# One decoder layer in float32 on one core: x's first blocks on ACT's queue, the last sums later, the stores in another order

## The chip, the cores and the metric

The kernel runs on 1 of the 8 cores of a Trainium2 chip. The metric is the device time of one execution in microseconds, the median of some runs. A core has five engines with a queue of instructions each: PE (matrix products), DVE and ACT (elementwise work), POOL and SP. Loads and stores are DMAs; SP and ACT issue them on hardware queues of their own (here called SP's and ACT's queue), POOL on a software queue. A DMA instruction stands in its engine's instruction stream like any other. SP does nothing but issue DMAs; ACT also computes.

## What is computed

One step of a hybrid decoder layer for 320 tokens: 256 of a prompt (two row tiles of 128) and 64 of a sample (8 sequences of 8), with D = 2048 columns, all in float32.

```python
def decoder_layer(x, conv_prev, k_win, v_win, rel_bias, w_in, w_conv, w_conv_out, sinks,
                  w_attn_out, w_o, g_mix, g_ffn, w_gate, w_up, w_down):
    xn = rms_norm(x, g_mix)
    z = xn @ w_in                       # B, C, h, q, k, v, gate_conv, gate_attn
    u = c_gate * h_conv
    y_conv = (b_gate * short_conv(u)) @ w_conv_out
    y_attn = window_attention(q, k, v, rel_bias, sinks) @ w_attn_out
    merged = jax.nn.sigmoid(gate_c) * y_conv + jax.nn.sigmoid(gate_a) * y_attn
    h = x + merged @ w_o
    hn = rms_norm(h, g_ffn)
    return h + (jax.nn.silu(hn @ w_gate) * (hn @ w_up)) @ w_down

y = rms_norm(h, g_final)                # and the new k, v and conv states
```

## The kernel before, in words

**Products.** Every product has the tokens as the moving side: a matmul takes a 128x128 block of weights and 128x320 of x, transposed so that the columns of x lie on partitions. To keep float32's precision, both sides are split in two parts of a shorter format: a weight tile `raw` becomes `hi` (a copy on ACT, L93) and `lo` (the rest, a subtraction on DVE, L94), x becomes `xh` and `xl` in the same way, and each product is three matmuls: hi by xh, hi by xl, lo by xh. `product` (L116) does that for all products but the first, with weight tiles that SP loads (`load_cols`, L96). Weights pass once: the kernel streams some 250 MB through four buffers of raw tiles and three each of `hi` and `lo`.

**The first product** is the one for k and v (`kv_product`, L267). It has four accumulators (c = 0 to 3) and sixteen steps kc, one for each 128 columns of x, with 12 matmuls a step. Its weight tiles are loaded by `load_kv` (L256) on SP: one step each for the first two (256 KB), then two steps each (512 KB).

**x.** The three row tiles `xs[t]` (two of the prompt, one of the sample) are loaded in five blocks of columns, `XB = [2, 2, 4, 4, 4]` times 128 columns, by `x_load(i)` (L223): three DMAs a block. In the following the load of block i and row tile t is x[i,t]; blocks 0 and 1 have 128 KB for a row tile of the prompt and 64 KB for the sample's, the others twice that. Block 0 is loaded ahead of all, x[0,1] on ACT's queue and the others on SP's; `g_mix`, as `vrow`, follows on ACT's. Blocks 1 to 4 are issued by `kv_product` on SP behind the weight tiles that `x_after` names. `x_prep(kc)` (L242) does what a step needs: three transposes on PE into one PSUM tile `pt`, then `xh` on ACT (scaled by `g_mix`), `xl` on DVE, and a plain copy `hT` on DVE for the residual. It is called for steps 0 and 1 at step 0, for 2 and 3 at step 1, then two steps ahead. Nine matmuls on constants (L235) keep PE busy before x is there.

**The order of the work.** The kernel is written with a layer that sets all semaphores and puts the instructions of each engine in order: of what is ready by its own reckoning, the earliest written goes first. `after(marks)` (L71) pins what is written under it behind a marked instruction of the same engine, in issue order only. Loads on the two hardware queues share eight completion semaphores, which are handed out in turn.

```python
with after(*((vecs_in,) if k0 == 0 else mark[k0])):
    split_to(hi[:, :n, :], lo[:, :n, :], raw[:, :n, :])
```

These two lines of `load_kv` (L263) pin the split of the first weight tile behind the copy of `g_mix`, and of every other behind the `xh` and `xl` of its first step. Side work (small loads on POOL, squares of x on ACT, the root of the mean square) is put between the tiles of the first product by `tick` (L111).

**The end.** The down product (w_down, `dn`) runs in two halves of its inner dimension. In the second half, each pair of column blocks is added to the residual `hT`, transposed back to rows (`fa`), squared with a row sum on ACT (`row_squares`, L908) into `ssf`, and scaled by `g_final` (`y_part`). The last pair differs. `next_last` (L923) treats column block 14 while PE still works on block 15, and sums the 15 row sums so far into `s15` (L932, L933). After the last matmul, block 15 is added in three parts (L966) and transposed (L967), row tile 0 is squared, and its inverse root `r0` is made (`row_mean`, `inv_root`: one root on ACT, a reciprocal and three small steps on DVE, the last three a Newton step). Row tiles 1 and 2 get theirs together (`r12`). Then all rows are scaled, in parts, by ACT and DVE (`scale`, L979; `scale_last`, L985, for the last two column blocks), and stored (`send`, L993): row tiles 0 and 1 from SP, the sample's 64 rows from ACT, last.

## Time and profile before

| | us |
|---|---|
| runs | 1701.84, 1702.18, 1702.85; median 1702.18 |
| the profiled execution | 1702.27 |
| its span, first to last instruction | 1700.5 |
| PE busy | 1682.2 (99%) |
| DVE, ACT, POOL busy | 863.3 (51%), 643.5 (38%), 81.3 (5%) |
| first matmul of the first product | 8.11 |
| from the last transposes to the end of the span | 13.3 |

A matmul of 128x320 is listed with 0.31 us, but matmuls are pipelined: one starts every 0.147 us while PE is the one that sets the pace (48 take 7.04 us in the chain of work). Idle time of an engine is listed with what ended it. A DMA is listed where it is issued (an engine's name with q), with the time that the issuing took; the time to landing is another view. The profile's clock is that which PE was granted, as a share of full speed. Its DMA numbers are the busy share of the core's 16 DMA engines and the rate in GB/s.

### The profile page before, as it was taken

What the parts mean: (1) busy time and instruction counts of PE and PEld (TensorE: products, weight loads), DVE (VectorE), ACT (ScalarE), POOL (GpSimd) and SP (SyncE); (2) the same over time, 40 slices, a digit from 0 to 9 for tenths busy, and PEclk for the clock granted to TensorE, in tenths of its full rate; (3) what the DMA queues carried; (4) which work ended last, traced back from release to release, by engine and by line L of the source; (5) the groups of instructions that cost most, each with busy time, mean ns of one, the idle gap of its engine ahead of it and who ended that gap; (6) DMA issues with size and microseconds to landing.
All of it is one profiled execution on the core that took longest, in us unless ns stands there. A gap on an engine that the chain in (4) does not pass through costs nothing.

```text
span 1700.5 us, 27713 instructions
## 1 busy us (share of the span) xinstructions
PE 1682.2 (99%) x11600; PEld 1670.9 (98%) x11600; DVE 863.3 (51%) x1231; ACT 643.5 (38%) x945; POOL 81.3 (5%) x127
## 2 busy tenths in 40 slices
PE   8999999999999999999999999999999999999996
PEld 7999999999999999999999999999999999999996
DVE  7667554444444445556454545433345545454443
ACT  6445443333333333334333333322233333333432
POOL 1001221000000001220000000000000000000000
PEclk9999999999999999999999999999999999999998
DMA  7754554555555544444444444444444444445442
GB/s 217 216 153 142 161 151 131 147 150 151 151 152 151 149 149 149 149 149 149 149 149 150 149 150 152 152 152 150 149 150 149 149 149 149 149 151 171 149 140 96
DMA packets 256719, 258.22 MB, mean 152 GB/s; under 512 B 9091, under 2 KB 251615, under 8 KB 256433
## 3 DMA queue, kind: packets, MB, share of 16 engines
q1 hardware_dynamic: 254128, 249.86, 47.8%
q0 software_dynamic: 2128, 5.92, 1.2%
q8 instruction: 91, 1.49, 0.4%
q10 hardware_dynamic: 336, 0.66, 0.2%
q14 instruction: 36, 0.29, 0.1%
HBM read 253.29 MB, written 5.08 MB: 152 GB/s over the span
## 4 chain that ended last, share of the span: by engine, by line
PE 95%; issue 2%; DMA 1%; DVE 1%; SPq 0%; POOL 0%; ACT 0%; DVEq 0%; POOLq 0%; ACTq 0%
PE fg L134 18%; PE fu L134 18%; PE dn L134 18%; PE wo L134 7%; PE ga L134 7%; PE gc L134 7%; PE C L134 3%; PE B L134 3%; PE H L134 3%; PE ya L134 3%; PE yc L134 3%; PE q L134 2%; DMA wraw<-in_w_in_dram 0%; DMA rel<-in_rel_bias_dram 0%; PE po L508 0%
## 5 line engine op out<-in xcount | busy, mean ns | idle before, releaser
L94 DVE TENSOR_TENSOR wlo<-wraw,whi 128x1024 fp32r<-128x1024 f32 (+1 forms) x481 | 573.8, 1195 | 703.9 <-ACT whi L93 701.3
L93 ACT ACTIVATE whi<-wraw 128x1024 fp32r<-128x1024 f32 (+1 forms) x481 | 493.3, 1030 | 852.4 <-PE dn L134 198.2
L134 PE MATMUL dn<-a_h,whi 128*128 128x320 f32 x704 | 218.5, 310 | 0.0
L134 PE MATMUL fu<-hh_t,whi 128*128 128x320 f32 x704 | 217.4, 309 | 0.0
L134 PE MATMUL dn<-a_h,wlo 128*128 128x320 f32 x704 | 217.3, 309 | 0.0
L134 PE MATMUL dn<-a_l,whi 128*128 128x320 f32 x704 | 217.2, 309 | 0.0
L134 PE MATMUL fg<-hh_t,whi 128*128 128x320 f32 x704 | 217.2, 309 | 0.0
L134 PE MATMUL fg<-hl_t,whi 128*128 128x320 f32 x704 | 217.2, 309 | 0.0
L134 PE MATMUL fg<-hh_t,wlo 128*128 128x320 f32 x704 | 217.2, 309 | 0.0
L134 PE MATMUL fu<-hl_t,whi 128*128 128x320 f32 x704 | 217.2, 308 | 0.0
L134 PE MATMUL fu<-hh_t,wlo 128*128 128x320 f32 x704 | 217.2, 308 | 0.0
L134 PEld LDWEIGHTS fu<-hl_t,whi 128*128 128x128 f32 x704 | 132.2, 188 | 0.1
L134 PEld LDWEIGHTS dn<-a_l,whi 128*128 128x128 f32 x704 | 132.2, 188 | 0.0
L134 PEld LDWEIGHTS fu<-hh_t,whi 128*128 128x128 f32 x704 | 132.2, 188 | 0.1
L134 PEld LDWEIGHTS dn<-a_h,whi 128*128 128x128 f32 x704 | 132.2, 188 | 0.0
L134 PEld LDWEIGHTS dn<-a_h,wlo 128*128 128x128 f32 x704 | 132.2, 188 | 0.0
L134 PEld LDWEIGHTS fg<-hh_t,whi 128*128 128x128 f32 x704 | 132.2, 188 | 0.0
L134 PEld LDWEIGHTS fg<-hh_t,wlo 128*128 128x128 f32 x704 | 132.2, 188 | 0.0
L134 PEld LDWEIGHTS fg<-hl_t,whi 128*128 128x128 f32 x704 | 132.2, 188 | 0.0
L134 PEld LDWEIGHTS fu<-hh_t,wlo 128*128 128x128 f32 x704 | 132.2, 188 | 0.0
L134 PE MATMUL gc<-xh_t,whi 128*128 128x320 f32 x256 | 79.6, 311 | 0.0
L134 PE MATMUL ga<-xh_t,wlo 128*128 128x320 f32 x256 | 79.4, 310 | 0.0
(285 smaller groups left out, 2934.7 us busy)
## 6 DMA issues: line engine op xcount, KB each, us to landing
wraw<-in_w_in_dram SPq DMA_DIRECT2D x119, 512.0 KB, 3.6
wraw<-in_w_gate_dram SPq DMA_DIRECT2D x88, 512.0 KB, 3.6
wraw<-in_w_up_dram SPq DMA_DIRECT2D x88, 512.0 KB, 3.6
wraw<-in_w_down_dram SPq DMA_DIRECT2D x88, 512.0 KB, 3.5
wraw<-in_w_o_dram SPq DMA_DIRECT2D x32, 512.0 KB, 3.5
wraw<-in_w_in_dram SPq DMA_DIRECT2D x34, 256.0 KB, 4.4
wraw<-in_w_conv_out_dram SPq DMA_DIRECT2D x16, 512.0 KB, 3.5
wraw<-in_w_attn_out_dram SPq DMA_DIRECT2D x32, 256.0 KB, 4.1
```

The source lines that it names most:

```text
L93: last["hi"] = nc.scalar.activation(hi, src, AF.Copy)
L94: last["lo"] = nc.vector.tensor_sub(lo, src, hi.bitcast(F32))
L134: last["mm"] = nc.tensor.matmul(ps[c][:, :T], w[:, k, c * P:(c + 1) * P], x(kc), start=(kc == 0 and i == 0), stop=(kc == nk - 1 and i == 2),)
```

## The change

It has two parts, one at each end of the kernel.

At the front, blocks 0, 1 and 2 of x are all loaded ahead of the first weight tile in the written order, and on ACT's queue, but for x[0,1], which is on SP's. ACT's queue now has nine loads: x[0,0], `vrow`, x[0,2], then the three of block 1 and of block 2. Blocks 3 and 4 stay on SP. There are seven warm-up matmuls instead of nine. `x_prep(0)` is called ahead of the first product's loop, `x_prep(1)` between the first and second accumulator of step 0, and `x_prep(kc + 2)` ahead of the last accumulator of step kc; the transposes of all but the first are pinned behind the matmul written last. The split of the first weight tile is now pinned behind `xh` and `xl` of step 0, like that of the others.

At the end, `s15` is summed after the three adds of block 15 instead of in `next_last`. The root of row tile 0 is written out, with one of its steps in another form but as many of them. The parts that are scaled and stored change: row tile 0 goes as 512, 512 and 1024 columns instead of 256, 768 and 1024; then the sample's rows, 768 and 1280 columns; then row tile 1, 768 and 1280. All stores are issued by SP.

```diff
--- before.py
+++ after.py
@@ -224,14 +224,17 @@
         cs = slice(sum(XB[:i]) * P, sum(XB[:i + 1]) * P)
         for t, (t0, tn) in enumerate(TOK):
             src = a["x_prompt"][0, t0:t0 + tn, :] if t < 2 else a["x_sample"].flatten_outer_dims()
-            eng = nc.scalar if i == 0 and t == 1 else nc.sync
+            eng = nc.sync if i > 2 or (i, t) == (0, 1) else nc.scalar
             eng.dma_start(xs[t][:tn, cs], src[:, cs])
-
-    x_load(0)
-    nc.scalar.dma_start(vrow[0:16, :], a["g_mix"][0].rearrange("(k p) -> k p", p=P))
+            if (i, t) == (0, 0):
+                nc.scalar.dma_start(vrow[0:16, :], a["g_mix"][0].rearrange("(k p) -> k p", p=P))
+
+
+    for i in range(3):
+        x_load(i)
 
     wm = ps_aux("wm")
-    for _ in range(9):
+    for _ in range(7):
         nc.tensor.matmul(wm, busy[:, :P], busy, start=True, stop=True)
     pv = ps_aux("pv")
     nc.tensor.transpose(pv[:, 0:16], vrow[0:16, :], ident[:16, :16])
@@ -241,8 +244,9 @@
 
     def x_prep(kc):
         pt = ps_aux(u("pt"))
-        for t in range(3):
-            nc.tensor.transpose(pt[:, t * P:(t + 1) * P], xs[t][:, kc * P:(kc + 1) * P], ident)
+        with after(*((last["mm"],) if kc else ())):
+            for t in range(3):
+                nc.tensor.transpose(pt[:, t * P:(t + 1) * P], xs[t][:, kc * P:(kc + 1) * P], ident)
         m1 = nc.scalar.activation(xh_t[:, kc, :], pt[:, :T], AF.Copy, scale=g_mix[:, kc:kc + 1])
         m2 = nc.vector.scalar_tensor_tensor(
             xl_t[:, kc, :], pt[:, :T], g_mix[:, kc:kc + 1], xh_t[:, kc, :].bitcast(F32),
@@ -260,13 +264,14 @@
         )
         hi = wp.tile([P, KT // 2, CK], F32R, tag="whi", name=u("whi"), bufs=3)
         lo = wp.tile([P, KT // 2, CK], F32R, tag="wlo", name=u("wlo"), bufs=3)
-        with after(*((vecs_in,) if k0 == 0 else mark[k0])):
+        with after(*mark[k0]):
             split_to(hi[:, :n, :], lo[:, :n, :], raw[:, :n, :])
         return hi, lo
 
     def kv_product(tiles, x_after):
 
         ps = [ps_acc(u("kv")) for _ in range(4)]
+        x_prep(0)
         k0 = 0
         for i, n in enumerate(tiles):
             hi, lo = load_kv(k0, n)
@@ -277,9 +282,8 @@
                 order.sort(key=lambda kc: kc[1])
             for k, c in order:
                 kc = k0 + k
-                if c == 0:
-                    for j in range(2 * kc, 2 * kc + 2) if kc < 2 else range(kc + 2, min(kc + 3, KC)):
-                        x_prep(j)
+                if (kc, c) == (0, 1) or c == 3 and kc + 2 < KC:
+                    x_prep(1 if c == 1 else kc + 2)
                 for m, (w, x) in enumerate(((hi, xh), (hi, xl), (lo, xh))):
                     last["mm"] = nc.tensor.matmul(
                         ps[c][:, :T], w[:, k, c * P:(c + 1) * P], x(kc),
@@ -363,7 +367,7 @@
         nc.vector.tensor_mul(rbsq, rb, rb)
 
     side_work[0] = start_rest()
-    ps_kv = kv_product([1, 1] + [2] * 7, {0: (1,), 1: (2,), 3: (3,), 4: (4,)})
+    ps_kv = kv_product([1, 1] + [2] * 7, {3: (3,), 4: (4,)})
     for _ in side_work[0]:
         pass
     for c in range(2):
@@ -929,8 +933,6 @@
                 nc.tensor.transpose(pc[0][:tn, t * P:(t + 1) * P], hT[:, k, t0:t0 + tn], ident)
             for t in range(3):
                 row_squares(t, k, pc[0])
-            nc.vector.tensor_reduce(s15, ssf[:, :, 0:KC - 1], axis=AX.X, op=ALU.add)
-            nc.vector.tensor_scalar(s15, s15, 1.0 / D, EPS, op0=ALU.mult, op1=ALU.add)
 
         pc = [None, None]
         for mp in range(8):
@@ -963,15 +965,11 @@
     k = KC - 1
     for t, (t0, tn) in enumerate(TOK):
         tr = slice(t0, t0 + tn)
-        nc.vector.tensor_add(hT[:, k, tr], hT[:, k, tr], ps[1][:, tr])
+        last["h"] = nc.vector.tensor_add(hT[:, k, tr], hT[:, k, tr], ps[1][:, tr])
         nc.tensor.transpose(pc[1][:tn, t * P:(t + 1) * P], hT[:, k, tr], ident)
-
-    def row_mean(ts):
-        vf = op.tile([P, ts.stop - ts.start], F32, name=u("vf"))
-        last["v"] = nc.vector.scalar_tensor_tensor(
-            vf, ssf[:, ts, KC - 1], 1.0 / D, s15[:, ts], op0=ALU.mult, op1=ALU.add
-        )
-        return vf
+    with after(last["h"]):
+        nc.vector.tensor_reduce(s15, ssf[:, :, 0:KC - 1], axis=AX.X, op=ALU.add)
+        last["s"] = nc.vector.tensor_scalar(s15, s15, 1.0 / D, EPS, op0=ALU.mult, op1=ALU.add)
 
     def rows(t):
         return y_p[0, t * P:(t + 1) * P, :] if t < 2 else y_s.flatten_outer_dims()
@@ -979,8 +977,9 @@
     def scale(eng, t, r, a0, a1):
         y = y_sb[t][:TOK[t][1], a0:a1]
         if eng is nc.scalar:
-            return nc.scalar.activation(y, y, AF.Copy, scale=r[:TOK[t][1]])
-        return nc.vector.tensor_scalar(y, y, r[:TOK[t][1]], None, op0=ALU.mult)
+            last["ya"] = nc.scalar.activation(y, y, AF.Copy, scale=r[:TOK[t][1]])
+        else:
+            last["y"] = nc.vector.tensor_scalar(y, y, r[:TOK[t][1]], None, op0=ALU.mult)
 
     def scale_last(t, r):
         tn = TOK[t][1]
@@ -994,41 +993,56 @@
         eng.dma_start(rows(t)[:, a0:a1], y_sb[t][:TOK[t][1], a0:a1])
 
     row_squares(0, k, pc[1])
-    r0 = inv_root(row_mean(slice(0, 1)), [P, 1], "rf", op)
+    v, g, r, q, r0 = (op.tile([P, 1], F32, name=u("rt")) for _ in range(5))
+    with after(last["s"]):
+        nc.vector.scalar_tensor_tensor(v, ssf[:, 0:1, KC - 1], 1.0 / D, s15[:, 0:1], op0=ALU.mult, op1=ALU.add)
+    last["root"] = nc.scalar.activation(g, v, AF.Sqrt)
+    nc.vector.reciprocal(r, g)
+    nc.vector.scalar_tensor_tensor(q, r, -0.5, r, op0=ALU.mult, op1=ALU.mult)
+    nc.vector.tensor_scalar(q, q, v, 1.5, op0=ALU.mult, op1=ALU.add)
     with after(last["root"]):
         for t in (1, 2):
             row_squares(t, k, pc[1])
-    with after(last["inv"]):
-        first = scale(nc.vector, 0, r0, 0, 256)
-    send(nc.sync, 0, 0, 256)
-    with after(last["root"]):
-        scale(nc.scalar, 0, r0, 256, 1024)
-    send(nc.sync, 0, 256, 1024)
-    with after(first):
+    last["y"] = nc.vector.tensor_scalar(r0, r, q, None, op0=ALU.mult)
+    with after(last["y"]):
+        scale(nc.vector, 0, r0, 0, 512)
+    send(nc.sync, 0, 0, 512)
+    scale(nc.scalar, 0, r0, 512, 1024)
+    send(nc.sync, 0, 512, 1024)
+    with after(last["y"]):
+        v, g, r, q, r12 = (op.tile([P, 2], F32, name=u("rt")) for _ in range(5))
+        last["y"] = nc.vector.scalar_tensor_tensor(
+            v, ssf[:, 1:3, KC - 1], 1.0 / D, s15[:, 1:3], op0=ALU.mult, op1=ALU.add
+        )
+    with after(last["ya"]):
+        last["root"] = nc.scalar.activation(g, v, AF.Sqrt)
+    with after(last["y"]):
+        scale(nc.vector, 0, r0, 1024, e0)
+    with after(last["y"]):
         scale_last(0, r0)
-    with after(last["y"]):
-        v12 = row_mean(slice(1, 3))
-    with after(last["v"]):
-        last["y"] = scale(nc.vector, 0, r0, 1024, e0)
     send(nc.sync, 0, 1024, D)
     with after(last["y"]):
-        r12 = inv_root(v12, [P, 2], "rf", op)
-    with after(last["inv"]):
-        r1, r2 = r12[:, 0:1], r12[:, 1:2]
-        last["a"] = scale(nc.scalar, 1, r1, 0, 640)
-        send(nc.sync, 1, 0, 640)
-        last["y"] = scale(nc.vector, 1, r1, 640, e0)
+        nc.vector.reciprocal(r, g)
+    nc.vector.scalar_tensor_tensor(q, r, -0.5, r, op0=ALU.mult, op1=ALU.mult)
+    nc.vector.tensor_mul(q, q, v)
+    last["y"] = nc.vector.scalar_tensor_tensor(r12, q, 1.5, r, op0=ALU.add, op1=ALU.mult)
+    r1, r2 = r12[:, 0:1], r12[:, 1:2]
+    with after(last["root"]):
+        scale(nc.scalar, 2, r2, 0, 768)
+    send(nc.sync, 2, 0, 768)
+    with after(last["y"]):
+        scale(nc.vector, 2, r2, 768, e0)
+    with after(last["y"]):
+        scale_last(2, r2)
+    send(nc.sync, 2, 768, D)
+    with after(last["ya"]):
+        scale(nc.scalar, 1, r1, 0, 768)
+    send(nc.sync, 1, 0, 768)
+    with after(last["y"]):
+        scale(nc.vector, 1, r1, 768, e0)
     with after(last["y"]):
         scale_last(1, r1)
-    send(nc.sync, 1, 640, D)
-    with after(last["a"]):
-        scale(nc.scalar, 2, r2, 0, 768)
-    send(nc.scalar, 2, 0, 768)
-    with after(last["y"]):
-        last["y"] = scale(nc.vector, 2, r2, 768, e0)
-    with after(last["y"]):
-        scale_last(2, r2)
-    send(nc.scalar, 2, 768, D)
+    send(nc.sync, 1, 768, D)
 
 
 _INS = ['x_prompt', 'x_sample', 'cache_k', 'cache_v', 'state_conv', 'rel_bias', 'w_in', 'w_conv',
```

## Prediction

> **What bounds the kernel now.** I read the busy table first, then the stretches of the span, the timeline of the first 17 us and of the last 14, the waits, and the loads with their time to landing.
>
> The stretches (columns: stretch, length, then busy time of each engine, granted clock, DMA share, GB/s) say where time can be won at all:
>
> ```profile
> 1.60:8.11 6.51, 5.03 (x19) 2.23 (x20) 4.08 (x8) 2.75 (x4) 0.00 (x0) 1.00 0.80 234
> 8.11:16.31 8.20, 6.20 (x42) 5.71 (x42) 3.96 (x7) 4.62 (x11) 2.10 (x5) 1.00 0.95 301
> 16.31:45.76 29.45, 29.45 (x208) 28.33 (x209) 24.39 (x53) 20.69 (x42) 5.19 (x11) 1.00 0.73 211
> 45.76:1687.20 1641.44, 1640.83 (x11332) 1634.26 (x11330) 824.53 (x1142) 611.58 (x878) 73.24 (x104) 1.00 0.49 150
> 1687.20:1700.50 13.30, 0.70 (x3) 0.38 (x3) 5.69 (x23) 3.87 (x11) 0.00 (x0) 0.63 0.58 197
> ```
>
> From 16.31 to 1687.20 us PE never stops. So a microsecond won or lost before 16.31 arrives whole at the end, and the 13.3 us of tail add to it. Nothing between is touched by the change. The start, as a timeline (start, length, engine, line, operation, idle time before):
>
> ```profile
> 0.74 0.41 ACTq L228 DMA_DIRECT2D x<-in_x_prompt_dram  x1
> ...
> 1.67 1.28 ACT L93 ACT_TABLE_LOAD   x1 [1.67 <-PEq L1061]
> ...
> 8.03 0.33 PE L245 MATMUL pt<-ident,x 128*128 128x128 f32 x1 [1.48 <-DMA x<-in_x_sample_dram]
> 8.11 0.83 PE L284 MATMUL kv<-xh_t,whi 128*128 128x320 f32 x4
> ...
> 12.66 0.47 SPq L228 DMA_DIRECT2D x<-in_x_sample_dram  x1
> ...
> 13.78 0.41 PE L284 MATMUL kv<-xh_t,whi 128*128 128x320 f32 x1 [1.24 <-ACT whi L93]
> ...
> 16.31 0.85 PE L284 MATMUL kv<-xh_t,wlo 128*128 128x320 f32 x4 [0.76 <-DVE wlo L94]
> ```
>
> The reader sees the three waits that the change is about: 1.48 us behind a late block of x, then 2.0 us behind the third weight tile, which landed at 12.65.
>
> **The front: when does the first product start?** Call its start T; it is 8.11 now. First the point at which nothing is won. Today product k runs from 8.11 until q starts at 45.76, 37.65 us, of which 2.0 are the two later waits. The change takes those away (weights no longer queue behind blocks 1 and 2 of x on SP), but two more groups of three transposes fall inside the product. One group costs 0.34 us (without it, three steps take 0.29 at 0.147 each; with it, 0.63 from 20.71 to 21.34), so 0.7. And the second weight tile is now split behind the second transpose: transpose 0.35, xh 0.51, whi 0.63 make 1.5 us, against 1.1 of PE work that is left beside it: a new wait of about 0.5. So q starts at T + 36.9, and the change wins at the front only if T is under 8.9.
>
> Now T. ACT's nine loads depend on nothing and stand ahead of every activation, as its two do in the timeline above, where the table load came behind them. So ACT converts nothing until the ninth is issued. At 0.41 to 0.58 us each that alone would end at 5.0. But a load can be held:
>
> ```profile
> SPq L258 <- DMA wraw<-in_w_in_dram: 0.9, 1, 0.9
> SPq L228 <- DMA wraw<-in_w_in_dram: 0.8, 1, 0.8
> SPq L228 <- DMA x<-in_x_sample_dram: 0.2, 1, 0.2
> ```
>
> These are SP's own waits. The load at 12.66 started as the tile issued at 6.00 landed (6.6 us later, below). Counting the loads of both queues in order, that one is the eighth before it. The loads at 11.54 and 14.06 likewise started as the eighth before each landed (11.5 and 14.0). So with both queues issuing in turn, ACT's fifth load (the second x tile of block 1) is the ninth of all and waits for the first, which lands 3.0 us after 0.74: it goes at 3.7, not 2.8. ACT's ninth is the seventeenth of all and waits for that fifth. When does the fifth land? Times to landing of single loads, and of two loads issued on a second queue:
>
> ```profile
> wraw<-in_w_in_dram SPq DMA_DIRECT2D x1, 256.0 KB, 4.7
> ...
> wraw<-in_w_in_dram SPq DMA_DIRECT2D x1, 512.0 KB, 6.6
> ...
> rel<-in_rel_bias_dram POOLq DMA_DIRECT2D x1, 2.0 KB, 5.9
> ...
> out_dram<-yb ACTq DMA_DIRECT2D x1, 192.0 KB, 4.3
> ```
>
> The first was issued at 3.91, beside our 3.7: that gives 8.4. By bytes it is later: 1480 KB stand ahead of it (x block 0, three weight tiles, one tile of block 1), and landings were 8.6 us at 1152 KB and 12.6 at 2304, so 1608 KB give 10.2; with the fourth weight tile ahead too, 2120 KB give 12.0. I take 9.3, between the two nearest rows; 8.4 and 12.0 stay as ends. The last two rows show that a second queue doesn't pass the first: 2 KB from POOL at 14.33 landed at 20.2 with what SP had issued before it, and ACT's 192 KB store took 4.3 us where SP's 128 KB took 2.0.
>
> The Trainium skill ("DMA: Bandwidth & Descriptors", section on queues, rings and completion order) has each engine take turns between queues packet by packet; the two rows speak against it. By that rule the sum would be 1703.9, the second rival's.
>
> Then: 9.3, ninth load 0.48, table load 1.28, xh 0.51, whi 0.63, gaps 0.05: T = 12.25, that is 3.35 us past the 8.9. Ends: 11.35 and 14.95, so 2.45 to 6.05.
>
> **The clock.** PE would idle from about 5.3 to 12.25. The trace has one such idle, the tail, where the clock halves 2.8 us after PE's last operation (1687.91 to about 1690.7), and one start:
>
> ```profile
> 4.14 0.15 PEld L235 LDWEIGHTS <-busy 128*128 128x128 bf16 x1 [0.28 <-issue]
> 4.56 0.10 PEld L235 LDWEIGHTS <-busy 128*128 128x128 bf16 x1 [0.27 <-issue]
> ...
> 1690.50:1691.00 0.50, 0.00 (x0) 0.00 (x0) 0.50 (x2) 0.26 (x2) 0.00 (x0) 0.72 0.22 76
> ```
>
> The weight loads shorten at 4.56, 2.9 us after PE's first operation at 1.60. So the product starts at half speed for about 2.9 us and loses 1.5, but then the new wait of 0.5 lies under the slow matmuls: 1.0. Ends: 0 (the clock holds) and 2.4 (two such stretches, 5.9 / 2 - 0.5). The two warm-up matmuls taken away (0.43 each) cost nothing, since ACT is what x waits for; without that cover they would shorten the warm PE's work by 0.9 us.
>
> **SP, POOL, DVE at the front.** SP loses eight loads (0.43 to 0.48 each), so the first weight tile goes at 1.2 instead of 1.82 and the third at 2.5 instead of 6.00: off the path while ACT is the one waited for. Blocks 3 and 4 of x wait for the weight tiles before them; block 3 is needed eight steps of over 2 us after T, so it is hidden. POOL's small loads wait for a conversion of block 3 of the columns and slide with T; they are used 7 us after they land (24.0, 31.7): nothing. DVE's order per step is unchanged: nothing.
>
> **The tail.** Moving the sums behind the three adds frees DVE at the end of the last matmul (1686.64): the first add goes at about 1686.70 instead of 1686.88, the third is no longer behind a sum.
>
> ```profile
> 1686.76 0.20 DVE L932 TENSOR_REDUCE s<-ssf 128x3 f32<-128x45 f32 x1 [1.68 <-ACT jk L911]
> 1686.88 0.28 DVE L966 TENSOR_TENSOR hT<-hT,dn 128x128 f32<-128x128 f32 x1
> 1687.07 0.16 DVE L933 TENSOR_SCALAR s<-s 128x3 f32<-128x3 f32 x1
> ```
>
> That is 0.2. The root has as many small steps as before (four, 0.2 each). From there on the tail moves 2560 KB of stores; the first is now 256 KB instead of 128, and at 318 GB/s in the stretch 1691 to 1692 against 419 in the next the stores were short of data for about 0.25. The last store goes at 1694.2 instead of 1694.33, as 640 KB at full width instead of 320 KB of half-width rows, but the half-width rows run at 227 GB/s wherever they stand. So 0.45 won. Ends: 0.9 won (no shortage at all, the last add earlier still), 0.4 lost (0.3 us without data before the sample's rows, which now wait for ACT's 0.92 us copy).
>
> **Sum** against the profiled execution, 1702.27 (span 1700.5 and 1.8 around it; the median of the three runs is 1702.18): 1702.27 + 3.35 + 1.0 - 0.45 = 1706.2. This case's own ends: + 2.45 + 0 - 0.9 = 1703.8, and + 6.05 + 2.4 + 0.4 = 1711.1.
>
> **The rivals.** First, on the other side: ACT converts the first block as soon as it lands, with its later loads behind. For it: what is ready could go first, if those loads stand held in the order. Against it: in the timeline both loads of ACT precede all else. Then x lands at 4.7 (with the first weight tile, 3.5 after 1.2), transpose to 5.1, xh 5.65, whi 6.2: T = 6.2, 2.7 won, with the tail 1699.1. It decides as soon as T is below 9.3. Second, queues that take turns: the fifth load then has 456 KB of its own queue and as much of SP's through it, 912 KB, where landings were 6.2 at 832 KB and 8.0 at 896: 7.0. T = 9.95, 1.05 lost, clock 1.0, tail 0.45: 1703.9. For it: at the very start ACT's and SP's blocks landed together; against it, the two rows above. Third, no load on ACT is held long: nine issues to 5.0, table load 6.3, two conversions: T = 7.4, 1.5 and 0.45 won: 1700.3. Against it, the three held loads of SP.
>
> **How the numbers follow.** Chances: the forecast 0.54, taking turns 0.12, converting first 0.18, no held loads 0.12, something slower yet (clock low for longer, a load past 12.0) 0.04. 0.2% is 3.4 us, about what a measurement of this kernel can tell from no change: the bounds are 1698.8 and 1705.7. Slower: 0.43 of the forecast's 0.54, 0.03 of taking turns, 0.04: 0.50. Faster: half of converting first (its tail or T at the good end), 0.09, and 0.01 of the third: 0.10. Within: 0.40. The range 1699.8 to 1709.6 leaves out most of converting first (0.14) and 0.06 at the top.
>
> **What would show it.** Right: ACT's first conversion stands behind its ninth load at about 11 us, PE waits some 7 us for it, the first kv matmul starts near 12.3 with steps of about 0.29 us, and the 1.24 and 0.76 us waits are gone. From the last dn matmul to the end, 0.45 less. Wrong: a conversion before ACT's last loads, or loads at even steps of 0.47 with no gap, or a fifth load that lands by 7; then T is under 10 and the change is worth nothing or wins. A clock that stays full takes 1.0 off.

## The result, and the profile after

The changed kernel takes 1707.82 us (median of nine runs, 1706.97 to 1708.33), beside 1702.7 us for the kernel before on the same chip: ratio 1.0029, with a 95% interval of 1.0019 to 1.0039. It is slower, by 5.1 us. The profiled execution took 1708.28 us (span 1706.5), 6.0 us above the profiled execution of before.

Four stretches carry the 6.0 us: up to the first kv matmul, from there to q, from q to the last dn matmul, and the tail. The stretches of the changed kernel (start and end, length, busy time of PE, its weight loads, DVE, ACT and POOL, granted clock, DMA share, GB/s; the second stretch is cut where the clock comes back):

```profile
1.60:9.60 8.00, 4.30 (x12) 1.49 (x12) 2.55 (x5) 2.33 (x3) 0.00 (x0) 0.96 0.93 281
9.60:15.79 6.19, 6.19 (x24) 6.06 (x25) 2.97 (x8) 2.62 (x5) 0.00 (x0) 0.50 1.05 312
15.79:50.26 34.47, 33.70 (x233) 31.51 (x231) 26.46 (x56) 23.23 (x49) 7.27 (x15) 1.00 0.60 167
50.26:1691.65 1641.39, 1640.56 (x11331) 1634.25 (x11330) 824.76 (x1139) 611.21 (x876) 73.26 (x104) 1.00 0.49 150
1691.65:1706.50 14.85, 0.95 (x6) 0.43 (x4) 6.41 (x25) 4.05 (x15) 0.00 (x0) 0.62 0.54 177
```

The product starts at 9.60 instead of 8.11 and runs its first 6.19 us at half clock. q starts at 50.26 instead of 45.76: 4.50 us of the loss is there by then. The last dn matmul starts at 1691.65 instead of 1686.33, so 0.8 more arises in between; the tail behind it takes 14.86 instead of 14.17, 0.7 more.

The start as a timeline (start, length, engine, line, operation, idle time before it), for the same places as before:

```profile
3.91 0.51 ACTq L228 DMA_DIRECT2D x<-in_x_sample_dram  x1
...
6.11 0.34 ACTq L228 DMA_DIRECT2D x<-in_x_prompt_dram  x1
6.22 0.30 PE L249 MATMUL pt<-ident,x 128*128 128x128 f32 x1 [0.62 <-DMA x<-in_x_sample_dram]
...
6.48 0.63 ACTq L228 DMA_DIRECT2D x<-in_x_sample_dram  x1
7.21 1.28 ACT L250 ACT_TABLE_LOAD   x1 [7.21 <-DMA x<-in_x_sample_dram]
8.50 0.53 ACT L250 ACTIVATE xh_t<-pt,vecs 128x320 fp32r<-128x320 f32 x1
8.93 0.62 ACT L93 ACTIVATE whi<-wraw 128x512 fp32r<-128x512 f32 x1
...
9.60 0.63 PE L288 MATMUL kv<-xh_t,whi 128*128 128x320 f32 x1 [3.08 <-ACT whi L93]
10.03 0.47 PE L288 MATMUL kv<-xl_t,whi 128*128 128x320 f32 x1
10.30 0.47 PE L288 MATMUL kv<-xh_t,whi 128*128 128x320 f32 x1
```

ACT does nothing but issue loads until 7.1. Its eighth load goes at 6.11, as its third one (the sample's rows of block 0, issued at 1.67) lands; the ninth follows at 6.48. Only then come the table load, xh and whi, and the first kv matmul behind them. The steps of the product are 0.27 us at first. PE's waits up to 80 us (total, times, longest):

```profile
PE kv L288 <- ACT whi L93: 3.1, 1, 3.1
...
PE q L134 <- DVE wlo L94: 0.8, 1, 0.8
PE kv L288 <- DVE wlo L94: 0.7, 1, 0.7
...
```

The old waits of 1.24 and 0.76 us for the third weight tile are gone. In their place stands one of 0.7 for a `wlo` at 41.73 (1.01 us from start to start of two matmuls that otherwise follow each other in 0.147), three small ones at 16, 22 and 26 us, and 0.8 in q.

The 4.50 us to the start of q, put together from these rows: the product starts 1.49 later; the two old waits go (-2.05, as gaps from start to start); two more groups of three transposes stand inside it (+0.68); 6.19 us at half speed hold 3.1 us of work less; the new waits for `wlo` make 1.4 (0.22 + 0.16 + 0.15 + 0.86). The sum is 4.6.

### The profile page after: what moved, and what is told of

It is laid out like the page before. It is cut to its first block, busy times and chain, and to the rows that moved or that the text cites. A ratio compares the mean times of both kernels' runs of the same rounds, so it can differ in the third digit from the quotient of the medians.

```text
span 1706.5 us, 27707 instructions
## 1 busy us (share of the span) xinstructions
PE 1685.7 (99%) x11598; PEld 1673.7 (98%) x11598; DVE 863.8 (51%) x1231; ACT 643.4 (38%) x945; POOL 81.3 (5%) x127
## 3 DMA queue, kind: packets, MB, share of 16 engines
q8 instruction: 91, 1.49, 0.4%
## 4 chain that ended last, share of the span: by engine, by line
PE 96%; DMA 1%; issue 1%; DVE 1%; ACT 0%; POOL 0%; DVEq 0%; ACTq 0%; POOLq 0%
PE dn L134 18%; PE fu L134 18%; PE fg L134 18%; PE wo L134 7%; PE gc L134 7%; PE ga L134 7%; PE C L134 3%; PE B L134 3%; PE H L134 3%; PE ya L134 3%; PE yc L134 3%; PE q L134 2%; PE kv L288 1%; DMA out_dram<-kn 0%; DMA wraw<-in_w_in_dram 0%
## 5 line engine op out<-in xcount | busy, mean ns | idle before, releaser
L134 PE MATMUL ga<-xh_t,whi 128*128 128x320 f32 x256 | 79.4, 310 | 0.0
```

What stands on the lines that cost most here:

```text
L134: last["mm"] = nc.tensor.matmul(ps[c][:, :T], w[:, k, c * P:(c + 1) * P], x(kc), start=(kc == 0 and i == 0), stop=(kc == nk - 1 and i == 2),)
```

## The experiments

Twelve kernels were run. Times are medians; the kernel before ran beside each, and the difference is to its median in the same series. First kv and q are the starts of the first matmul of each product, the tail runs from the start of the last dn matmul to the end; these three are of one profiled execution. The front of the kernel before was profiled three times (before, a2, c1): first kv came at 7.22 to 8.11 and q at 45.76 to 46.53, so a difference under 1 us in these two columns doesn't by itself show an effect of an edit. Where the texts speak of transposes of a block, a block has the 128 columns of one `x_prep`; a block of a load has 256 or 512 columns, as before.

| kernel | us | against before | 95% interval of the ratio | first kv | q | tail |
|---|---|---|---|---|---|---|
| before | 1702.2 to 1702.7 | | | 8.11 | 45.76 | 14.17 |
| the whole change | 1707.82 | +5.1 | 1.0019 to 1.0039 | 9.60 | 50.26 | 14.86 |
| a1 front alone | 1706.84 | +4.4 | 1.0017 to 1.0036 | 9.72 | 50.13 | 14.20 |
| a2 tail alone | 1703.13 | +0.7 | 0.9994 to 1.0012 | 7.22 | 46.03 | 14.87 |
| a3 loads alone | 1704.44 | +2.0 | 1.0000 to 1.0019 | 9.56 | 47.27 | 14.23 |
| a4 transposes alone | 1705.27 | +2.8 | 1.0008 to 1.0027 | 7.95 | 48.36 | 14.14 |
| b1 PE kept at work | 1706.16 | +3.5 | 1.0012 to 1.0031 | 9.49 | 48.32 | 14.85 |
| b2 table load early | 1706.01 | +3.4 | 1.0012 to 1.0031 | 8.47 | 48.58 | 14.84 |
| b3 block 2 on SP | 1705.58 | +3.0 | 1.0006 to 1.0025 | 7.84 | 48.50 | 14.87 |
| b4 transposes earlier | 1705.90 | +3.3 | 1.0009 to 1.0028 | 9.61 | 48.37 | 14.83 |
| c1 row tile 1 first | 1702.49 | +0.1 | 0.9990 to 1.0009 | 7.48 | 46.53 | 14.05 |
| c2 loads apart | 1700.11 | -2.3 | 0.9975 to 0.9993 | 7.00 | 43.43 | 13.95 |
| d1 ten warm-ups | 1707.56 | +5.0 | 1.0017 to 1.0041 | 9.39 | 50.05 | 14.80 |
| d2 before, seven warm-ups | 1701.46 | -1.1 | 0.9985 to 1.0004 | 6.43 | 44.94 | 14.15 |

### The parts alone

**a1**, the new front with the old tail, and **a2**, the old front with the new tail (the diff of the change, cut at `next_last`).

> The new front (loads on ACT's queue, seven warm-up matmuls, transposes inside the first product) with the old tail. Reading of the trace after the change: the q product starts 4.5 us later, its first weights cost 0.8 us more, and the tail is a cost of its own of 0.7 us. Then this kernel takes 5.3 us more than the kernel before, the first kv matmul stands at 9.6 us, and from the last dn matmul to the end it takes 14.2 us. Rival, as predicted: the new tail saves 0.45 us, so this kernel is 0.45 us slower than the whole change and its tail is longer than the 14.9 us of the whole change.

> The old front with the new tail. Reading of the trace after the change: q starts at 45.8 us as before, jk of row tile 0 starts 0.26 us sooner behind the last dn matmul, and the end comes 0.7 us later behind it (14.9 us against 14.2 us), since the sample's 64 rows are sent alone in the middle and row tile 1 goes last: 0.7 us slower than before. Rival, as predicted: 0.45 us faster than before. Second rival: the longer tail came from the later front (another state of the clock at the end), and the tail is 14.2 us or less.

The two differences, +4.4 and +0.7, add up to the whole's +5.1, and both tails are as the theory had them: 14.20 and 14.87 us. a2's +0.7 by itself isn't clear of noise (its interval holds 1), but the tails are: the seven executions with the new one take 14.80 to 14.87, the five with the old one 14.14 to 14.23. So the tail loses 0.7 by itself, whatever the front does. a1 also tells that the 0.8 us wait in q is no part of the change: a1 has the same instructions there and doesn't show it. PE's waits list it with 0.8 to 1.1 us in the profiled executions of the whole change, a3 and b1, with 0.3 to 0.5 in b4, d1 and d2, and not in the others. What brings it stays open. Without it the profiled execution of the whole change would stand 5.2 above before, close to the medians' 5.1.

**a3**, only the loads and the seven warm-ups:

```diff
-            eng = nc.scalar if i == 0 and t == 1 else nc.sync
+            eng = nc.sync if i > 2 or (i, t) == (0, 1) else nc.scalar
...
-    x_load(0)
+    for i in range(3):
+        x_load(i)
...
-    ps_kv = kv_product([1, 1] + [2] * 7, {0: (1,), 1: (2,), 3: (3,), 4: (4,)})
+    ps_kv = kv_product([1, 1] + [2] * 7, {3: (3,), 4: (4,)})
```

> Only the loads move to ACT's queue (and two warm-up matmuls go); the transposes of blocks 0 and 1 stay ahead of the first product, the tail is the old one. Theory (ACT's own loads hold up its conversions): ACT's first activation comes at 7.2 us again behind the ninth load, whi, xh and xh follow the table load, the first kv matmul stands at 9.7 to 10.3 us, the clock halves from 9.0 us on, the waits of 1.24 and 0.76 us are gone, and q starts 3.5 to 5.5 us later than in the kernel before. Rival (the moved transposes carry the loss): q starts within 1.5 us of the kernel before.

**a4**, only the transposes:

```diff
-        for t in range(3):
-            nc.tensor.transpose(pt[:, t * P:(t + 1) * P], xs[t][:, kc * P:(kc + 1) * P], ident)
+        with after(*((last["mm"],) if kc else ())):
+            for t in range(3):
+                nc.tensor.transpose(pt[:, t * P:(t + 1) * P], xs[t][:, kc * P:(kc + 1) * P], ident)
...
-        with after(*((vecs_in,) if k0 == 0 else mark[k0])):
+        with after(*mark[k0]):
...
+        x_prep(0)
...
-                if c == 0:
-                    for j in range(2 * kc, 2 * kc + 2) if kc < 2 else range(kc + 2, min(kc + 3, KC)):
-                        x_prep(j)
+                if (kc, c) == (0, 1) or c == 3 and kc + 2 < KC:
+                    x_prep(1 if c == 1 else kc + 2)
```

> Only the transposes move into the first product; loads, warm-up matmuls and tail are the old ones. Theory (the loads carry the loss): ACT converts from 5.4 us on, the first kv matmul stands at 7 to 8.5 us, the clock stays full, q starts within 1.0 us of the kernel before (45.8 us), and the whole is within 1.5 us of it. Rival (the transposes pinned between the products make the weights' halves late): new waits of PE for wlo of 1.4 us in the first product and 0.8 us in q appear here too, and it is 2 us slower.

The theory that the loads carry the loss falls. a3 delays the first product as foretold, in the timeline:

```profile
7.17 1.28 ACT L93 ACT_TABLE_LOAD   x1 [7.17 <-DMA x<-in_x_sample_dram]
8.46 0.63 ACT L93 ACTIVATE whi<-wraw 128x512 fp32r<-128x512 f32 x1
...
9.56 0.90 PE L287 MATMUL kv<-xh_t,whi 128*128 128x320 f32 x2 [2.27 <-ACT xh_t L249]
```

but q starts only 1.5 later than before, for from there on the product has no wait at all: 37.7 us from its first matmul to q, of which 4.6 were stepped at 0.267 us. The transposes lose more, 2.8. a4's timeline and waits up to 80 us:

```profile
5.55 1.28 ACT L247 ACT_TABLE_LOAD   x1 [5.55 <-DVE vecs L238]
6.85 0.53 ACT L247 ACTIVATE xh_t<-pt,vecs 128x320 fp32r<-128x320 f32 x1
7.27 0.62 ACT L93 ACTIVATE whi<-wraw 128x512 fp32r<-128x512 f32 x1
7.95 0.64 PE L285 MATMUL kv<-xh_t,whi 128*128 128x320 f32 x1 [2.21 <-ACT whi L93]
8.38 0.47 PE L285 MATMUL kv<-xl_t,whi 128*128 128x320 f32 x1
```

```profile
PE kv L285 <- ACT whi L93: 2.6, 2, 2.2
PE kv L285 <- DVE wlo L94: 1.3, 2, 0.7
```

Three things show. The split of the first weight tile, which the kernel before did ahead of the conversions of x, now comes last of a chain, table load, xh, whi. PE, which has only one block's transposes to do meanwhile, idles 2.2 us, and the product starts at half clock (the rows at 8.38 and after it step by 0.267). And the waits for `wlo` are there.

### What stands behind the front's loss

Each of these takes one suspected cost out of the whole change.

**b1**, PE kept at work:

```diff
-    for _ in range(7):
+    for _ in range(9):
...
         x_prep(0)
+        with after(last["pt"]):
+            for _ in range(12):
+                nc.tensor.matmul(wm, busy[:, :P], busy, start=True, stop=True)
```

(`last["pt"]` is the last transpose of `x_prep`.)

> The whole change, with PE kept at work ahead of the first product: nine warm-up matmuls in place of seven, and twelve more behind the transposes of block 0. Theory (the halved clock is the largest part of the front's loss): the first kv matmul stays at 9.6 to 9.9 us, the kv matmuls step by 0.148 us from the start or nearly so, q starts at 47 to 48 us (50.3 in the whole change), and the whole comes out 2.2 to 3.2 us below it, some 2 us above the kernel before. Rival (the products wait for the conversions behind the same blocked engine anyway, and the slow clock is hidden): q starts at 49.5 us or later, and the gain is under 1 us.

**b2**, the table load ahead of ACT's last loads:

```diff
+            if (i, t) == (2, 0):
+                nc.scalar.activation(act0, ones[:, 0:1], AF.Copy)
```

> The whole change, with one activation of 128x1 on a constant put behind the seventh of ACT's nine loads, so that ACT's table load stands there. Theory (the table load of 1.28 us lies in the path only because it stands behind all nine loads; ACT waits at the eighth load until 6.1 us anyway): the table load runs from 4.6 to 5.9 us, the eighth and ninth load go out as before (6.1 and 6.5 us), the first kv matmul stands at 8.2 to 8.4 us, and the whole is 1.3 to 3 us below the whole change (more than 1.3 if the clock then comes back sooner). Rival (the loads behind the table load go out later by 1.3 us): the first kv matmul stays at 9.4 us or later and nothing is gained.

**b3**, block 2 back on SP:

```diff
-            eng = nc.sync if i > 2 or (i, t) == (0, 1) else nc.scalar
+            eng = nc.sync if i > 1 or (i, t) == (0, 1) else nc.scalar
...
-    ps_kv = kv_product([1, 1] + [2] * 7, {3: (3,), 4: (4,)})
+    ps_kv = kv_product([1, 1] + [2] * 7, {1: (2,), 3: (3,), 4: (4,)})
```

> The whole change, with the three loads of block 2 given back to SP's queue at their old place, so that ACT issues six loads, none of which is held for another. Theory (what sets ACT's first activation is its own loads, the eighth and ninth above all): ACT is free at 4.4 us, the table load is over by 5.7 us, xh follows the last transpose of block 0 (6.5 us), the first kv matmul stands at 7.4 to 8.0 us, and the whole is 1.5 to 4 us below the whole change; waits for the third or fourth weight tile may come back (2.0 us in the kernel before). Rival (the hold is not ACT's, but the sample's block that lands at 6.1 us behind the weights): the first kv matmul stays at 9 us or later.

**b4**, the transposes of blocks 4 to 15 nine matmuls sooner:

```diff
-                if (kc, c) == (0, 1) or c == 3 and kc + 2 < KC:
+                if (kc, c) == (0, 1) or c == (3 if kc < 2 else 0) and kc + 2 < KC:
```

> The whole change, with the transposes of blocks 4 to 15 pinned nine matmuls (1.3 us) sooner, at the first quarter of the block two ahead, where the kernel before had them; blocks 1 to 3 stay inside the first product. Theory (transposes pinned late make xh, and behind it the weights' halves, late): the waits of PE for wlo of 0.16, 0.15 and 0.86 us at 22, 26 and 42 us go, and q starts 1.0 to 1.3 us sooner than in the whole change, if the clock does the same. Rival (these waits come from ACT's table load and its other work alone, however the transposes stand): the wait of 0.86 us stays and less than 0.4 us is gained.

Each mechanism is there. In b1 the product runs at full clock from its first step (9.49). In b2 the first kv matmul stands 1.1 sooner, at 8.47, a little later than expected. In b3, whose ACT has six loads (the sixth was held until 4.00, and ACT was done with them at 4.5),

```profile
5.27 1.28 ACT L250 ACT_TABLE_LOAD   x1 [5.27 <-DVE vecs L241]
...
7.84 0.63 PE L288 MATMUL kv<-xh_t,whi 128*128 128x320 f32 x1 [1.14 <-ACT whi L93]
```

the table load comes 1.94 and the product 1.76 sooner; what it waits for is now the copy of `g_mix`. So ACT's own loads did hold up its conversions. In b4 PE waits for nothing from 17 to 60 us, where the whole change has its 0.7: the late transposes made the weights' halves late. Its clock also came back 2.5 us sooner, at 13.31, but by a1 and d1, taken up below, that alone gains next to nothing.

But the four gain 1.7 to 2.2 us and no more, and q starts between 48.32 and 48.58 in all of them, whether the product began at 7.84 or at 9.61. In b1 the lines that show why:

```profile
12.69 1.05 ACT L93 ACTIVATE whi<-wraw 128x1024 fp32r<-128x1024 f32 x1
13.70 1.82 DVE L94 TENSOR_TENSOR wlo<-wraw,whi 128x512 fp32r<-128x512 f32 x2
...
14.44 0.42 PE L291 MATMUL kv<-xh_t,wlo 128*128 128x320 f32 x1 [0.56 <-DVE wlo L94]
```

The third weight tile landed at 8.96 in this execution, and is split from 12.69: it stands behind the conversions of blocks 1 and 2, whose transposes wait inside the product for PE. A part of what b1 wins on the clock it waits for there. b3 has the same wait at 14.62. Executions with the whole new front tell the same: a1 and d1 ran 3.2 and 4.9 us of the product at half speed, the whole change 6.2, but q starts at 50.13, 50.05 and 50.26. Where the clock came back sooner, PE waited longer for the `wlo` of the third tile at 16 us, 0.7 and 0.8 instead of 0.2. The costs of the front aren't a sum of terms; where one goes, the next takes a part of its place.

**d1** and **d2**, the warm-ups by themselves: ten instead of seven in the whole change, and seven instead of nine in the kernel before.

> The whole change with ten warm-up matmuls in place of seven, and nothing else. In the profiled executions so far the clock rose before 5.6 us in all six kernels with nine or ten warm-ups at the start, and in one of six with seven (the whole change itself). Theory (the number of warm-ups decides whether the clock rises before the first product, but the gap behind them, to 9.6 us, loses it again): the clock rises at 4.4 to 5.6 us, drops at 7.8 to 9.0 us or one window later, q starts at 48.3 to 50.3 us, and the whole is 0 to 1.5 us below the whole change. Rival (with ten it holds through the gap): q starts at 47 to 48.3 us and the whole is 2 us or more below.

> The kernel before with seven warm-up matmuls in place of nine, and nothing else. Theory (two warm-ups fewer lose the rise of the clock in most executions): the first kv matmuls step by 0.267 us, the clock rises at 9.5 to 14.2 us, the waits of 1.24 and 0.76 us take up a part of the loss, and the whole is 0.3 to 1.5 us slower than before. Rival, as priced in the prediction (two warm-ups fewer cost nothing): within 0.2 us of before, with the clock up by 5.6 us.

This theory falls on both sides. In d1 the product still starts at half speed and the whole is as slow as the change:

```profile
9.39 0.64 PE L288 MATMUL kv<-xh_t,whi 128*128 128x320 f32 x1 [2.30 <-ACT whi L93]
10.10 0.47 PE L288 MATMUL kv<-xh_t,whi 128*128 128x320 f32 x1
```

In d2 the clock rises at 6.0, and the kernel is no slower; its 1.1 us below before lie within the interval. So two warm-ups fewer cost nothing that can be measured. What goes with the half clock is PE's wait for ACT's conversions: in all eight kernels in which it comes to 1.1 to 3.1 us ahead of the product the product starts at half speed, in the six others (before, a2, b1, c1, c2, d2) at full. In two of the eight, the whole change and a4, the clock had risen and fell again; in six it had not risen by then. The last section tells what the clock follows.

### The tail, and a version that uses what was found

**c1**: the old front, and the new tail with the last two parts exchanged.

```diff
     with after(last["root"]):
-        scale(nc.scalar, 2, r2, 0, 768)
-    send(nc.sync, 2, 0, 768)
+        scale(nc.scalar, 1, r1, 0, 768)
+    send(nc.sync, 1, 0, 768)
...
```

> The old front with the new tail, but with row tile 1 scaled and sent ahead of the sample's rows (all on SP's queue still). Theory (the new order is what lengthens the tail: the sample's 64 rows run alone at 115 to 283 GB/s in the middle, and 1 MB of row tile 1 waits behind them): from the last dn matmul to the end 14.2 us or less (14.87 with the sample's rows ahead). Rival (the split of row tile 0's sends or the one queue lengthens it): 14.7 to 15 us again.

The stretches of the last 6 us show it. The whole change, and then c1 (1 us each; the last column is GB/s):

```profile
1699.00:1700.00 1.00, 0.00 (x0) 0.00 (x0) 0.53 (x3) 0.00 (x0) 0.00 (x0) 0.50 0.84 178
1700.00:1701.00 1.00, 0.00 (x0) 0.00 (x0) 0.00 (x0) 0.00 (x0) 0.00 (x0) 0.50 1.02 226
1701.00:1702.00 1.00, 0.00 (x0) 0.00 (x0) 0.00 (x0) 0.00 (x0) 0.00 (x0) 0.50 0.95 153
1702.00:1703.00 1.00, 0.00 (x0) 0.00 (x0) 0.00 (x0) 0.00 (x0) 0.00 (x0) 0.50 0.93 366
1703.00:1704.00 1.00, 0.00 (x0) 0.00 (x0) 0.00 (x0) 0.00 (x0) 0.00 (x0) 0.50 1.06 433
```

```profile
1694.50:1695.50 1.00, 0.00 (x0) 0.00 (x0) 0.55 (x3) 0.00 (x0) 0.00 (x0) 0.50 1.07 418
1695.50:1696.50 1.00, 0.00 (x0) 0.00 (x0) 0.00 (x0) 0.00 (x0) 0.00 (x0) 0.50 1.02 410
1696.50:1697.50 1.00, 0.00 (x0) 0.00 (x0) 0.00 (x0) 0.00 (x0) 0.00 (x0) 0.50 1.00 316
1697.50:1698.50 1.00, 0.00 (x0) 0.00 (x0) 0.00 (x0) 0.00 (x0) 0.00 (x0) 0.50 1.09 228
```

With the sample's rows in the middle, these run by themselves from 1699 to 1702. Row tile 1, whose two sends are issued at 1699.57 and 1700.19, comes behind them, a megabyte at the end. With row tile 1 first the rate stays at 410 to 418 until it is out, and the half-width rows come last: the tail is 14.05, 0.8 shorter, and 0.1 under the old tail.

The half-width rows themselves aren't much slower in the middle. The whole change, and then the kernel before, where they come last:

```profile
1699.50:1701.50 2.00, 0.00 (x0) 0.00 (x0) 0.03 (x1) 0.00 (x0) 0.00 (x0) 0.50 1.10 218
```

```profile
1696.50:1698.50 2.00, 0.00 (x0) 0.00 (x0) 0.00 (x0) 0.00 (x0) 0.00 (x0) 0.50 1.07 236
```

What the place costs lies on both sides of them. In half microseconds, the rate is 262 and 154 from 1698.5 to 1699.5, where their two sends, issued at 1698.05 and 1698.97, are only starting, and 90 and 313 from 1701.5 to 1702.5, before row tile 1 is at full rate. An estimate from these rows: 0.845 MB moved from 1698.5 to 1702.5; with the sample's 0.524 MB at 218 GB/s and the rest at 420 that takes 3.2 us, and it took 4.0. Why the rate falls behind the rows, with row tile 1's first send issued two microseconds earlier, stays open.

**c2** puts together what the runs showed: block 2 back on SP behind the third weight tile, so that ACT is done with its loads at 4.4; the first two blocks' transposes ahead of the product and the next four inside it; ten warm-ups; and the old order of sends with the sums moved.

```diff
-            eng = nc.scalar if i == 0 and t == 1 else nc.sync
+            eng = nc.sync if i > 1 or (i, t) == (0, 1) else nc.scalar
...
-    x_load(0)
+    for i in range(2):
+        x_load(i)
...
+        with after(*((last["mm"],) if 2 <= kc < 6 else ())):
...
-                if c == 0:
-                    for j in range(2 * kc, 2 * kc + 2) if kc < 2 else range(kc + 2, min(kc + 3, KC)):
-                        x_prep(j)
+                if c == 0 and kc == 0:
+                    x_prep(0)
+                    x_prep(1)
+                elif (kc, c) in ((1, 1), (1, 2), (2, 3), (3, 2)) or kc > 3 and c == 0 and kc + 2 < KC:
+                    x_prep(kc + c if kc == 1 else kc + 2)
...
-    ps_kv = kv_product([1, 1] + [2] * 7, {0: (1,), 1: (2,), 3: (3,), 4: (4,)})
+    ps_kv = kv_product([1, 1] + [2] * 7, {2: (2,), 3: (3,), 4: (4,)})
...
+    with after(last["h"]):
+        nc.vector.tensor_reduce(s15, ssf[:, :, 0:KC - 1], axis=AX.X, op=ALU.add)
+        nc.vector.tensor_scalar(s15, s15, 1.0 / D, EPS, op0=ALU.mult, op1=ALU.add)
```

> A version made from what the runs showed. Front: of x only blocks 0 and 1 go through ACT's queue (six loads), block 2 through SP's behind the third weight tile; ten warm-up matmuls; the transposes of blocks 0 and 1 stay ahead of the first product, those of blocks 2 to 5 are pinned inside it, and the others stand where they stood. Tail: the old one, with the last sums on DVE behind the three additions. Theory (loads are no loss when ACT is held by none of them, PE keeps its clock, and the transposes aren't late): the first kv matmul stands at 6.8 to 7.4 us, PE waits less than 0.7 us in the first product, q starts at 42.5 to 44.5 us (45.8 before), jk of row tile 0 starts 0.26 us sooner behind the last dn matmul and the tail is 13.9 us; in all 1.5 to 3.5 us faster than before. Rival (the weights and x can't land any sooner, whichever queue they take: the product is bound by its loads): q starts at 45 us or later and the whole is within 0.8 us of the kernel before.

It takes 1700.11 us (1699.79 to 1700.55), 2.3 us less than before: faster than both kernels, though by 0.14%. The theory's numbers hold, the tail (13.95) included. Its stretches from the first kv matmul to q, and its waits from 6 to 80 us:

```profile
7.00:16.31 9.31, 8.81 (x60) 8.45 (x61) 6.84 (x14) 6.60 (x14) 3.94 (x7) 1.00 0.98 310
16.31:43.43 27.12, 27.12 (x193) 25.88 (x192) 22.62 (x50) 18.96 (x39) 4.00 (x9) 1.00 0.78 217
```

```profile
PE kv L290 <- ACT whi L93: 0.5, 1, 0.5
PE kv L290 <- ACT xh_t L250: 0.3, 1, 0.3
...
```

By 16.31 the product has been at work for 9.31 us with 0.5 us of waiting, where the kernel before had 8.20 with 2.0. So the front can be made shorter with x and weights on two queues, in a form in which ACT's conversions don't stand behind loads that are held until 6 us: q starts 2.3 to 3.1 us sooner than in the three executions of the old front, and 1.5 sooner than in d2. Which of c2's edits at the front carries how much of it was not tried apart.

## Why the prediction was right and wrong

The forecast, 1706.2 us, lies 1.6 below the measured 1707.82, with the right sign. Several of its terms were wrong, and they cancelled: it had q start at 12.25 + 36.9 + 1.0 = 50.15, and q started at 50.26. That the time came so near is luck. With the measured 9.60 in place of 12.25 its sum gives 1703.5; the 2.65 us too many on the loads covered what it had too low in the clock (by 2.1), the waits for `wlo` (0.9) and the tail (1.1). One of its own signs of being wrong came true, "a fifth load that lands by 7", and what it drew from that was wrong as well: T was under 10, and the change still lost 5.1.

- **ACT converts nothing until its ninth load is issued.** Right: the table load stands at 7.21, behind all nine. b3 and c2 show it from the other side, with the table load at 5.27 and 4.41 behind six. The rival in which ACT converts first is out.
- **A load waits for the eighth before it, over both queues.** Right in kind: ACT's eighth load went as its third landed, and that one is the eighth before it over both queues in the order in which the semaphores were handed out (a weight tile was issued 0.02 us ahead of it). Wrong in the count. The step "with both queues issuing in turn" failed: SP was itself held at its fourth load (4.08, as the first block of x landed), so ACT's eighth and ninth were the 13th and 14th of all, not the 15th and 17th, and the ninth didn't wait for the fifth at all but went at 6.48. The fifth landed at 6.62 instead of 9.3, since the third and fourth weight tile, which the sum had ahead of it, were held back as well. First kv 9.60 instead of 12.25: the term measured +0.70 instead of +3.35, below its lower end of 2.45.
- **The break-even, q at T + 36.9.** The two waits did go, and the groups of transposes did cost 0.7. Wrong was what the pinned transposes cost, "DVE's order per step is unchanged: nothing" and a new wait of 0.5. Measured were 1.4 of waits for `wlo`, 0.86 of it far behind the front, at 41.73. There ACT's second table load stands ahead of a weight split that the late transpose had pushed back:

```profile
37.43 0.53 ACT L250 ACTIVATE xh_t<-pt,vecs 128x320 fp32r<-128x320 f32 x1 [0.83 <-PE pt L249]
37.98 1.28 ACT L185 ACT_TABLE_LOAD   x1
...
39.38 1.04 ACT L93 ACTIVATE whi<-wraw 128x1024 fp32r<-128x1024 f32 x1
...
40.45 1.23 DVE L94 TENSOR_TENSOR wlo<-wraw,whi 128x1024 fp32r<-128x1024 f32 x1 [0.77 <-ACT whi L93]
```

  b4, with the transposes nine matmuls sooner, has none of the three waits at 22, 26 and 42 us.
- **The clock.** Right that it halves, wrong in size: 6.19 us of the product at half speed, 3.1 us, where the sum had 1.0 and its upper end 2.4. The step "the product starts at half speed for about 2.9 us" took the time from PE's first work at the kernel's start to the rise. The last section shows why that isn't a constant. As b1 shows, of the 3.1 some 1.7 come back when the clock is kept; the rest would then be waited for.
- **Two warm-ups fewer cost nothing.** Right (d1, d2), and without the cover that was named: d2 has none, and isn't slower.
- **Nothing between is touched.** Right by a1: the 0.8 us in q comes and goes with the execution.
- **The tail.** The first step was right: jk of row tile 0 starts 1.42 us behind the last dn matmul instead of 1.68, and in c2, with the old sends, the whole tail gains 0.22. But the first store goes 3.66 us behind it, as before (3.67), since it now has 512 columns instead of 256. The step on the sends failed, the one that concluded from "the half-width rows run at 227 GB/s wherever they stand" that their place is free. The rate did nearly hold, 218 GB/s in the middle beside 236 at the end, but the stores ran short on both sides of the rows, and what this held up was the last megabyte: +0.69 instead of -0.45, beyond the end of +0.4. "0.3 us without data before the sample's rows" was seen, as an end; the gap behind them was not.

The rival by the Trainium skill ("DMA: Bandwidth & Descriptors", queues, rings and completion order), with T at 9.95 and 1703.9 in all, came near the measured start of 9.60, and its fifth load, at 7.0, near the 6.62. But the queues didn't take turns evenly, in bytes or in packets: from 2.0 to 4.5 us, with loads waiting on both, SP's queue moved 0.58 MB in 372 packets and ACT's 0.16 MB in 203. The sample's 64 KB, issued on ACT at 1.67 with 136 KB ahead of them on that queue, landed at 6.09, behind all of SP's first 640 KB (5.62). What made T early was the count of loads, by which SP was held as well.

## What to carry to other kernels

A queue of an engine that also computes is not free: its loads stand ahead of its computation, and one that is held for an earlier landing holds the computation too; count the loads of all queues together, with the holds of each, before pricing it. A step that is moved inside a product to start it earlier moves everything that is chained behind it, up to the next table load. Store the full-width rows first and leave the narrow ones for the end, when nothing waits behind them.

## What was unexpected of the hardware

The moments at which the granted clock changes lie whole multiples of 3.413 us apart within an execution, and at no fixed place of the program. In the whole change it rose at 5.55, fell at 8.96 and rose at 15.79 us; in c1 it was full from 4.36, fell at 14.60 and rose at 18.02. The stretches of the whole change between such moments:

```profile
5.55:8.96 3.41, 0.35 (x2) 0.14 (x1) 0.00 (x0) 1.74 (x3) 0.00 (x0) 1.00 0.96 278
8.96:12.37 3.41, 2.77 (x10) 2.73 (x11) 1.55 (x3) 0.59 (x2) 0.00 (x0) 0.50 1.02 360
12.37:15.79 3.42, 3.42 (x15) 3.33 (x15) 1.96 (x5) 2.62 (x5) 0.00 (x0) 0.50 1.06 271
```

After 0.35 us of PE work in one such stretch the clock halved. 2.77 us in the next didn't bring it back, and the 3.42 of a full one did. In c1 it halved after a stretch with 1.51 us of work. Counted over all fourteen profiled executions, in stretches of 3.413 us laid out from these moments, full clock ended 17 times, each time after a stretch with 1.79 us of PE work or less (1.79 in d1, from 1690.27 to 1693.69), and went on after every one with 1.84 or more (1.84 in a2, from 11.20 to 14.62). So here a little over half a stretch of work kept the clock, and less lost it. A product that starts behind a gap can run close to two such stretches at half speed: the one that it fills only in part, and the next.

The Trainium skill ("TensorE: Matmul & The Clock Gate", the part on the clock gate) states a window of 3.413 us that runs on freely and isn't set to the kernel's start. The trace agrees, with 3.413 us and with rises at 4.4 to 6.0 us where the warm-ups brought one. The Trainium skill has the clock fall after an idle window (same page, same part). Here up to 1.79 us of work in a window weren't enough to hold it, and there the measurement decides.

How much work a window needs to raise the clock stays open: 2.78 us of it, warm-ups and what follows them, raised it in a2 at 4.38, while 3.01 us from 4.09 to 7.51 in d1 didn't, if its windows are counted back from its rise at 14.33.
